# Tree attention on one core: another order for the first pairs, and copies moved between VectorE, ScalarE and GpSimd

## The chip, the cores and the metric

The kernel runs on one core of one Trainium2 chip. The metric is the device time of one execution in microseconds, the median of several runs. One core has a TensorE (PE in the profile; PEld is its loading of weights), a VectorE (DVE), a ScalarE (ACT), a GpSimd (POOL), a SyncE (SP) and 16 DMA engines. GpSimd's own DMA queue can convert fp32 to bf16 on the way. The queues of SyncE and ScalarE, called hardware queues here, are used without converting.

## The reference, cut to what matters

```python
batch, heads, seq, dim = 8, 12, 512, 64
for i in range(seq):                      # node i sees itself and its ancestors in a binary tree
    mask[i, i] = 1
    parent = i
    while parent > 0:
        parent = (parent - 1) // 2
        mask[i, parent] = 1
scores  = np.einsum('bhqd,bhkd->bhqk', Q, K) / sqrt(dim) + (1 - mask) * (-1e9)
weights = softmax(scores)
out     = np.einsum('bhqk,bhkd->bhqd', weights, V)   # fp32
```

There are 96 heads of 512 queries by 64. A node has at most nine ancestors. So a query needs its scores against the nodes near the root, and against a few blocks of keys in which its lower ancestors lie; most of the 512 by 512 scores are never computed.

## The kernel before, in words

The heads go in 48 pairs (`NP`), four pairs to a group of eight heads (`GP = 4`, `KB = 8`, 12 groups), and V in blocks of 16 heads (`VB`, 6 blocks). Group 0 has another layout of its loads than groups 1 to 11, which are called coarse in the code. A pair passes these stages:

- **Loads.** GpSimd issues them: `load_k`, `load_q`, `load_v`, each for eight heads as a rule, fp32 in memory and bf16 on the chip. Three tiles each are kept of K and Q (8 heads) and of V (16 heads). Only K and Q of heads 0 and 1 come as fp32 by the queues of SyncE and ScalarE (`first_load`, line 185) and are cast by VectorE (line 758).
- **Laying beside.** For groups 3 to 11 the two halves of K and of Q are copied so that heads of a pair lie beside each other (`lay_beside`, line 319, tiles Kbeside and Qbeside, two buffers each). A transpose then covers 128 rows. Q is always laid by GpSimd; K of groups 3, 4 and 5 by VectorE in turns 7, 10 and 14 (`K_TURN`), K of groups 6 to 11 by GpSimd.
- **Transposes** on TensorE (`T`, lines 359, 384 and 406) into the PSUM tile kqp, of which there is one, and its evacuation by VectorE (`evac`, lines 445, 453 and 459). In a coarse group two of the four transposes are of keys, two of queries, and the last two are evacuated together (line 445).
- **Scores** (`S`): the near-root tile (`scores1`) and the lower blocks (`scores2`), each with a matmul that adds the mask's codes; ScalarE takes the exponentials (lines 519 and 550).
- **Spreading V** (`spread`, line 309): V's rows are copied into the tile vt in the order in which the scores' columns stand. It has ten parts (0 to 9) for each block of V; parts 6 to 9 are the near-root tile. Three engines share these copies, by tables: `BY_VECTOR`, `BY_SCALAR`, and `spread_top` in GpSimd's program.
- **Values** (`V`, line 561) into the PSUM tile ob, of which there is one, then the reciprocal and the product on VectorE (`norm`, lines 594 and 599).
- **Stores** by GpSimd, eight heads each (`store`, line 607); the last four pairs singly (`store_pair`), the last two of them by the hardware queues.

The order on TensorE is written out: `FIRST` gives the steps of turns 0 to 5, one letter each; from then on a turn is `STV`, with an extra transpose in turn 9 (`TWICE`). `X` is a matmul on zeros that fills time, `K` and `Q` are the two halves of a transpose, `D` and `A` place the copies of that turn's tables. In turn i the scores of pair i and the values of pair i - 1 are issued; the transposes run some pairs ahead. What GpSimd does is a list made by `pool_program`; `pool` takes operations off its head as soon as a rule (`ready`) allows them to be issued. All engines work through their own instructions in order and wait for each other by semaphores.

Of the kernel before, what the change touches and what calls it, by code (L numbers as in the profile page):

```python
# [11 lines left out]
CODE_ROWS = 40  # L12
CODE_BITS = 16
NOUT = 10
BEHIND = 64
LANES = 8
COARSE = range(1, 12)
COARSE_K = range(1, 12)
BESIDE = {"K": range(3, 12), "Q": range(3, 12)}
K_BY_POOL = range(6, 12)  # L20


UNITS = (
# [101 lines left out]
def kernel(  # L125
# [59 lines left out]
    def first_load(eng, name, src):  # L185
        eng.dma_start(
            out=first[name][:, :, :, :].rearrange("p h t d -> p h (t d)"), in_=src[:, 0:2, :]
        )

    first_load(nc.sync, "K", Kr)  # L190
    nc.scalar.dma_start(out=ptile[:, :], in_=perm_dram.ap())
    first_load(nc.scalar, "Q", Qr)
# [58 lines left out]
    issued = {(name, h) for name in ("kst", "qst") for h in (0, 1)}  # L251
    qTs, kTs, kqps, obs, ets, ofs = {}, {}, {}, {}, {}, {}

    def load(kept, pool, name, size, src, h0, n):
# [52 lines left out]
            src = vst[0:32, h0:h1, UNITS[TOP + j][1], :]  # L307
            dst = vt[32 * j:32 * j + 32, h0:h1, 0, 0:w]
        return copy(out=dst, in_=src)  # L309

    def spread_top(o, h0=0, h1=VB):
        for part in range(6, 10):
            spread(nc.gpsimd.tensor_copy, o, part, h0, h1)
        for part in ((), (4, 5), (4, 5), (4, 5, 2))[min(o, 3)]:
            spread(nc.gpsimd.tensor_copy, o, part, h0, h1)

    besides = {}

    def lay_beside(copy, name, g):

        kept = (ksts if name == "K" else qsts)[g]
        to = besides[name, g] = beside.tile([P, GP, 4, 2, D], bf16, name=f"{name}beside")
        dst = to[:, :, :, :, :].bitcast(mybir.dt.uint32)
        src = kept[:, :, :, :].bitcast(mybir.dt.uint32)
        if g not in COARSE:
            src = src.rearrange("p (x a) t w -> p x t a w", a=2)
        elif name == "Q" or g in COARSE_K:
# [5 lines left out]
        copy(out=dst, in_=src)  # L333
# [284 lines left out]
            in_=ofs[i][:, a:a + n, :, :].rearrange("p h t d -> p h (t d)"),  # L618
        )

    def pool_program():

        K_BEFORE = {
            6: (load_k, 8 * KB, KB), 10: (spread_top, 5, 0, KB), 11: (store, nc.gpsimd, 5),
        }

        Q_BEFORE = {
            3: (load_k, 5 * KB, KB), 4: (load_k, 6 * KB, KB), 5: (spread_top, 3, 0, KB), 6: (spread_top, 3, KB, VB),
            9: (spread_top, 4, KB, VB), 10: (spread_top, 5, KB, VB),
        }  # L630
        ops = [
            (load_k, 2, 2), (load_q, 2, 2), (load_v, 0, 8), (load_k, 4, 4),
            (load_q, 4, 2), (load_q, 6, 2), (load_k, 8, 8), (load_q, 8, 8), (eye_order,),
            (load_v, 8, 8), (code_order, 0), (code_order, 64),
            (load_k, 16, 8), (load_q, 16, 8), (load_v, 16, 8),
            (load_k, 24, 8), (load_q, 24, 8), (load_v, 24, 8),
            (load_k, 32, 8), (spread_top, 0, KB, VB), (spread_top, 1, 0, KB),
            (load_v, 32, 8), (load_q, 32, 8), (load_k, 40, 8),
            (spread_top, 1, KB, VB),
        ]  # L640
        stored = 0
        for h in range(40, NH, KB):
            if h == 40:
                ops += [(load_v, h, KB), (load_q, h, KB)]
            else:
                ops += [(load_k, h, KB), (load_q, h, KB)]
            if h + KB < NH:
                ops.append((load_v, h + KB, KB))
            if h % VB == KB:
                ops.append((spread_top, h // VB, 0, KB))  # L650
            elif h >= 48:
                ops.append((spread_top, h // VB - 1, KB, VB))
            while KB * stored + KB + BEHIND <= h + KB:
                ops.append((store, nc.gpsimd, stored))
                stored += 1
        ops.append((spread_top, NH // VB - 1, KB, VB))
        ops += [(store, nc.gpsimd, q) for q in range(stored, NH // KB - 1)]
        ops += [(store_pair, nc.gpsimd, i) for i in (NP - 4, NP - 3)]
        for g in BESIDE["Q"]:
            if g in Q_BEFORE:  # L660
                ops.insert(ops.index(Q_BEFORE[g]), (lay_q, g))
                continue
            at = ops.index((load_q, KB * g, KB)) + 1
            behind = 0
            while behind < LANES:
                behind += {load_k: 1, load_q: 1, load_v: 1, store: 2, store_pair: 1}.get(ops[at][0], 0)
                at += 1
            ops.insert(at, (lay_q, g))
        for g in K_BY_POOL:
            before = K_BEFORE.get(g, (lay_q, g))  # L670
            ops.insert(ops.index(before), (lay_early, g))
        return ops

    def ready(op, i):

        f, args = op[0], op[1:]
        if f in (load_k, load_q):
            g = args[0] // KB - 3
            name = "K" if f is load_k else "Q"
            return (name, g) in besides if g in BESIDE[name] else done >= GP * (g + 1)  # L680
        if f in (code_order, eye_order):
            return True
        if f in (lay_q, lay_early):
# [3 lines left out]
        if f is spread_top:  # L687
            return 2 * i >= VB * (args[0] + 1 - NV)
        if f is store_pair:
            return i > args[1]  # L690
        return i >= GP * (args[1] + 1)

    BY_VECTOR = {
# [15 lines left out]
    }  # L709
    BY_SCALAR = {  # L710
        0: [(0, 8, 0, 4), (0, 1, 0, 4), (0, 4, 0, 4), (0, 5, 0, 8)],
        2: [(0, 9, 4, 8)],
        4: [(0, 1, 8, 16), (0, 2, 8, 16)],
        8: [(1, 2, 0, 8)],
        12: [(1, 2, 8, 16)],
        15: [(2, 1, 0, 8)],
        18: [(2, 1, 8, 16)],
    }

# [26 lines left out]
                out=tile[:, 0, :], lhsT=idle[:, 0:128], rhs=idle[:, :], start=True, stop=True  # L746
            )

    def lay_k(i):

        for g in BESIDE["K"]:
            if g not in K_BY_POOL and i == K_TURN.get(g, GP * g - 7):
                lay_beside(nc.vector.tensor_copy, "K", g)

    spin("s1", 9)
    for kept, name, src in ((ksts, "kst", "K"), (qsts, "qst", "Q")):
        kept[0] = loads.tile([P, KB, 4, D], bf16, name=name)
        nc.vector.tensor_copy(out=kept[0][:, 0:2, :, :], in_=first[src][:, :, :, :])
    TWICE = (9,)
    K_TURN = {3: 7, 4: 10, 5: 14}  # L760
    FIRST = ['XKSQ', 'SXXXKXQDVAT', 'SVATT', 'SVTT', 'STV', 'STVD']
    done = 1
    pool(-1)
    transpose(0)
    evac(0)
    valued = False
    for i in range(NP + 1):
        steps = FIRST[i] if i < len(FIRST) else "STVT" if i in TWICE else "SVT" if i == 8 else "STV"
        for n, step in enumerate(steps):
            if step == "S" and i < NP:  # L770
                scores1(i)
                scores2(i)
            if step == "V" and i >= 1:
                values(i - 1)
                norm(i - 1)
                valued = True
            if step == "T" and done < NP:
                transpose(done)
                evac(done)
                done += 1  # L780
                if "T" not in steps[n + 1:]:
                    lay_k(i)
            if step == "K":
                transpose(done, (0,))
            if step == "Q":
                transpose(done, (1,))
                evac(done)
                done += 1
            if step == "X":
                spin("s1" if valued else "ob", 2)  # L790
            if step == "D":
                spread_by(nc.vector.tensor_copy, BY_VECTOR, STEADY_VECTOR, i)
            if step == "A":
                spread_by(nc.scalar.copy, BY_SCALAR, STEADY_SCALAR, i)
        if "D" not in steps:
            spread_by(nc.vector.tensor_copy, BY_VECTOR, STEADY_VECTOR, i)
        if "A" not in steps:
            spread_by(nc.scalar.copy, BY_SCALAR, STEADY_SCALAR, i)
        if "T" not in steps:
            lay_k(i)  # L800
        pool(i)
        if i == NP - 1:
            store_pair(nc.sync, NP - 2)
    assert not program
# [32 lines left out]
```

## Time and profile before

| | |
|---|---|
| median of 3 runs | 132.94 us (132.73 to 133.97) |
| profiled execution: span | 131.9 us |
| profiled execution: own time | not shown apart from the span; the median lies 1.04 us above it |
| TensorE busy | 115.4 us (88%) |
| VectorE busy | 99.8 us (76%) |
| GpSimd busy | 96.0 us (73%) |
| ScalarE busy | 94.1 us (71%) |
| read from and written to HBM | 37.86 MB and 12.58 MB |
| granted TensorE clock | 0.993 |

The profile is of one execution. Times in it count from the first instruction. A line of the timeline has start, length, engine, line of the code, operation, what it writes and reads, the number of instructions merged, and in brackets the idle time before it with what ended that. In a line of the windows stand start:end, length, and for each engine the busy time with the number of instructions, then the granted clock, the busy share of the DMA engines (over 1 where packets overlap), and what they moved in GB/s.

### The profile page before, as it was taken

Reading aid. Unit: us, or ns where it says so; the run is one execution under the profiler, and the core shown is the slowest. Engines: PE = TensorE matmul, PEld = TensorE weight load, DVE = VectorE, ACT = ScalarE, POOL = GpSimd, SP = SyncE. Lnnn points to the kernel's source line nnn. Section 1 sums busy time; section 2 is a strip of 40 time slices with the busy share of each in tenths; the row PEclk is TensorE's granted clock in tenths of the full one; section 3 lists DMA queues with packets and bytes.
Section 4 is the critical chain, followed back from the end, with each engine's and each line's share of the span. In section 5 each row is a group of like instructions: output and inputs, shape, how many; then the busy total and the mean of one; then the engine's idle time right before and its main releaser. Section 6 shows DMA issues by size and latency. Waiting matters only on the chain.

```text
span 131.9 us, 4944 instructions
## 1 busy us (share of the span) xinstructions
PE 115.4 (88%) x2130; PEld 82.4 (62%) x2131; DVE 99.8 (76%) x191; ACT 94.1 (71%) x154; POOL 96.0 (73%) x147
## 2 busy tenths in 40 slices
PE   4989968899799879699999998999999999989930
PEld 1443645667566657477777776786877777856620
DVE  4339957774996897987988979879888799775460
ACT  4339345797766695778977889587888897979910
POOL 6999546049589899999999999699699998202300
PEclk9999999999999999999999999999999999999997
DMA  3999999999999999999999999999999989999991
GB/s 115 201 181 194 212 195 217 195 211 204 208 200 211 205 208 201 211 202 212 205 207 207 220 342 221 208 341 228 209 325 245 299 352 391 370 381 404 375 366 66
DMA packets 24533, 32.13 MB, mean 244 GB/s; under 512 B 944, under 2 KB 15920, under 8 KB 24512
## 3 DMA queue, kind: packets, MB, share of 16 engines
q0 software_dynamic: 23232, 30.67, 110.2%
q1 hardware_dynamic: 720, 0.70, 1.6%
q10 hardware_dynamic: 560, 0.46, 1.1%
q8 instruction: 16, 0.26, 0.7%
q14 instruction: 5, 0.04, 0.1%
HBM read 37.86 MB, written 12.58 MB: 382 GB/s over the span
## 4 chain that ended last, share of the span: by engine, by line
PE 63%; DVE 25%; ACT 6%; issue 3%; ACTq 0%
PE ob L561 18%; PE s L503 8%; PE kqp L406 8%; DVE of L599 7%; DVE kq L445 6%; PE s L508 6%; PE kqp L384 6%; PE s L528 6%; PE s L534 5%; DVE vt L309 4%; PE s L745 3%; ACT e L550 3%; ACT e L519 2%; PE kqp L359 2%; DVE kq L453 2%
## 5 line engine op out<-in xcount | busy, mean ns | idle before, releaser
L519 ACT ACTIVATE e<-s 128x1024 bf16<-128x1024 f32 x48 | 49.1, 1023 | 28.1 <-PE s L508 27.9
L309 POOL COPY vt<-vst 32x256 uint32<-32x256 uint32 (+2 forms) x70 | 36.1, 516 | 10.1 <-DMA vst<-in_V_dram 6.9
L550 ACT ACTIVATE e<-s 128x384 bf16<-128x384 f32 (+1 forms) x92 | 41.4, 505 | 0.0
L561 PE MATMUL ob<-vt,e 128*128 128x65 bf16 (+1 forms) x940 | 37.3, 197 | 3.2 <-DVE of L599 2.4
L561 PEld LDWEIGHTS <-e 128*128 128x128 bf16 (+1 forms) x960 | 31.2, 102 | 9.4 <-DVE of L599 4.8
L599 DVE TENSOR_TENSOR of<-ob,rec 128x512 f32<-128x512 f32 x44 | 30.4, 691 | 1.5
L309 DVE COPY vt<-vst 32x512 uint32<-32x512 uint32 (+4 forms) x43 | 23.2, 539 | 1.2
L594 DVE RECIPROCAL rec<-ob 128x8 f32<-128x8 f32 x47 | 9.5, 203 | 14.3 <-PE ob L561 13.5
L534 PEld LDWEIGHTS <-kq 64*128 64x128 bf16 x384 | 16.1, 110 | 6.4
L508 PE MATMUL s<-kq 64*128 64x512 bf16 x96 | 18.4, 378 | 1.3 <-DVE kq L445 1.3
L534 PE MATMUL s<-kq 64*128 64x160 bf16 (+1 forms) x384 | 17.8, 210 | 0.0
L503 PE MATMUL s<-qcoarse,codes 40*128 40x512 bf16 x88 | 17.2, 387 | 0.0
L528 PE MATMUL s<-qcoarse,codes 40*128 40x480 bf16 x88 | 16.3, 364 | 0.4 <-ACT e L550 0.2
L453 DVE COPY kq<-kqp 128x1024 bf16<-128x1024 bf16 x22 | 15.1, 687 | 2.0 <-PE kqp L384 1.3
L607 POOL DMA_DIRECT2D out_dram<-of x11 | 9.8, 893 | 8.5 <-DVE of L599 8.5
L445 DVE COPY kq<-kqp 128x2048 bf16<-128x2048 bf16 x11 | 13.5, 1224 | 2.4 <-PE kqp L406 1.8
L528 PEld LDWEIGHTS <-codes 40*128 40x128 bf16 x96 | 7.5, 95 | 9.1 <-issue 2.0
L384 PE MATMUL kqp<-mixed,Kbeside 128*128 128x128 bf16 x144 | 11.1, 220 | 1.8 <-DVE Kbeside L333 1.2
L333 POOL COPY Qbeside<-qst 128x1024 uint32<-128x1024 uint32 x9 | 9.7, 1081 | 2.6 <-DMA qst<-in_Q_dram 2.5
L406 PE MATMUL kqp<-ptile,Qbeside 128*128 128x128 bf16 x144 | 11.1, 220 | 0.4 <-DVE kq L453 0.4
L260 POOL DMA_DIRECT2D vst<-in_V_dram x12 | 10.9, 907 | 0.0
L384 PEld LDWEIGHTS <-Kbeside 128*128 128x128 bf16 x144 | 8.3, 98 | 3.2 <-DVE Kbeside L333 1.5
(45 smaller groups left out, 97.7 us busy)
## 6 DMA issues: line engine op xcount, KB each, us to landing
out_dram<-of POOLq DMA_DIRECT2D x11, 1024.0 KB, 9.9
vst<-in_V_dram POOLq DMA_DIRECT2D x12, 512.0 KB, 14.4
kst<-in_K_dram POOLq DMA_DIRECT2D x11, 512.0 KB, 12.2
qst<-in_Q_dram POOLq DMA_DIRECT2D x11, 512.0 KB, 13.2
out_dram<-ol POOLq DMA_DIRECT2D x2, 256.0 KB, 5.3
qst<-in_Q_dram POOLq DMA_DIRECT2D x3, 128.0 KB, 7.6
ol<-in_K_dram SPq DMA_DIRECT2D x1, 256.0 KB, 2.9
ol<-in_Q_dram ACTq DMA_DIRECT2D x1, 256.0 KB, 3.6
```

Source lines behind the costliest of these rows:

```text
L309: return copy(out=dst, in_=src)
L384: nc.tensor.transpose(out=dst, in_=src, identity=perm)
L406: nc.tensor.transpose(out=dst, in_=src, identity=eye[:, 0:128])
L445: return nc.vector.tensor_copy(out=dst, in_=src) if x == 3 else None
L503: nc.tensor.matmul(out=columns(g, sp[:, a, :], 0, 512), lhsT=k1code[64 * a:64 * a + CODE_ROWS, :], rhs=query_codes(i, a, 0, 0, 512), start ...
L508: nc.tensor.matmul(out=columns(g, sp[:, a, :], 0, 512), lhsT=keys(i, a, TOP), rhs=queries(i, a, 0, 512), start=False, stop=True,)
L519: nc.scalar.activation(out=dst, in_=src, func=AF.Exp, scale=scale)
L528: nc.tensor.matmul(out=columns(g, flat[:, a, :], 32, 512), lhsT=k2code[64 * a:64 * a + CODE_ROWS, :], rhs=query_codes(i, a, 1, 32, 512), s ...
L534: nc.tensor.matmul(out=columns(g, flat[:, a, :], lo, hi), lhsT=keys(i, a, TILE2[t]), rhs=queries(i, a, lo, hi), start=False, stop=t == 1,)
L550: nc.scalar.activation(out=dst, in_=src, func=AF.Exp, scale=scale)
L561: nc.tensor.matmul(out=ob[lo:hi, a, 65 * t:65 * t + 65], lhsT=e[:, a, PLACE[t], lo:hi], rhs=vt[:, head(i, a) % VB, tile_v, 0:D + 1], **flags,)
L599: nc.vector.tensor_tensor(out=dst, in0=o4[:, a:a + n, :, 0:D], in1=rec[:, a:a + n, :, :].to_broadcast([P, n, 4, D]), op=ALU.mult,)
```

## The change

It replaces the generated program of GpSimd and the tables by others:

- K and Q of heads 2 and 3 come as fp32 by the queues of SyncE and ScalarE and are cast by ScalarE; GpSimd's first load is V of heads 0 to 7, then K and Q of heads 4 to 7, four heads at a time.
- The first pairs have another order on TensorE: pair 0's values come after the scores of pair 2 instead of pair 1, and the filling matmuls behind the first are gone.
- The near-root parts (6 to 9) of the first eight heads of V are copied by GpSimd, no longer by VectorE and ScalarE.
- Part 3 of V blocks 1 and 2 goes from VectorE to ScalarE.
- K of groups 3 and 5 is laid by GpSimd instead of VectorE; K of group 4 stays on VectorE in turn 10.
- The extra transpose of turn 9 moves to turn 17, and turn 8 has the usual order.
- GpSimd's list is written out. The loads of K, Q and V of the last groups stand earlier in it, the stores later: the first store comes behind the last load of V.

```diff
-    for name, src in (("K", Kr), ("Q", Qr)):
-        first[name] = olast.tile([P, 2, 4, D], fp32, name="ol")
+    for h in (0, 2):
+        for name in "KQ":
+            first[name, h] = olast.tile([P, 2, 4, D], fp32, name="ol")
...
     nc.sync.dma_start(out=codes[0:CODE_BITS, :], in_=code_dram.ap())
+    first_load(nc.sync, "K", 2)
+    first_load(nc.scalar, "Q", 2)
...
+    POOL = (
+        "v0 k4.4 q4.4 k8 q8 v8 e c0.6.0.8 c0.7.0.8 c0.8.0.8 c0.9.0.8 x0 x64 k16 q16 v16 k24 q24 v24 "
+        "k32 t0.8 t1.0 K3 v32 q32 Q3 k40 t1.8 v40 q40 v48 t2.0 "
+        "Q4 k48 q48 v56 K5 t2.8 k56 q56 v64 Q5 t3.0 K6 k64 q64 v72 Q6 t3.8 "
+        "k72 q72 K7 Q7 v80 k80 q80 t4.0 v88 s0 K8 Q8 k88 q88 t4.8 s1 K9 Q9 t5.0 s2 K10 s3 Q10 t5.8 s4 K11 Q11 s5 s6 s7 s8 s9 s10 p44 p45 "
+    )
...
     BY_VECTOR = {
-        0: [(0, 0, 0, 8), (0, 7, 0, 8), (0, 2, 0, 8), (0, 6, 0, 8), (0, 9, 0, 4), (0, 3, 0, 8), (0, 8, 4, 8)],
-        1: [(0, 4, 4, 8)],
-        2: [(0, 1, 4, 8)],
+        0: [(0, 0, 0, 8), (0, 2, 0, 8), (0, 3, 0, 8)],
+        1: [(0, 1, 0, 8), (0, 4, 0, 8)],
         3: [(0, 4, 8, 16), (0, 5, 8, 16)],
         4: [(0, 3, 8, 16), (0, 0, 8, 16)],
-        7: [(1, 1, 0, 8), (1, 3, 0, 8)],
+        7: [(1, 1, 0, 8)],
...
     BY_SCALAR = {
-        0: [(0, 8, 0, 4), (0, 1, 0, 4), (0, 4, 0, 4), (0, 5, 0, 8)],
-        2: [(0, 9, 4, 8)],
+        0: [(0, 5, 0, 8)],
         4: [(0, 1, 8, 16), (0, 2, 8, 16)],
+        7: [(1, 3, 0, 8)],
...
-    K_TURN = {3: 7, 4: 10, 5: 14}
-    FIRST = ['XKSQ', 'SXXXKXQDVAT', 'SVATT', 'SVTT', 'STV', 'STVD']
+    EARLY = "CK CQ X K S Q D0 S A0 T D1 S T V S V T T V T T S D3 A3 T V S D4 A4 T V D5"
+    TURNS = {8: 'S T V', 10: 'S T L4 V', 17: 'S T V T'}
```

In GpSimd's list k, q, v are loads by their first head; e and x are the orders of the constants; c is one spread copy (block, part, heads); t is all of GpSimd's spread copies for eight heads of a block; K and Q lay a group beside; s and p are stores. In `EARLY`, C casts a load of heads 2 and 3 on ScalarE, and L4 lays K of group 4 on VectorE.

More of the change, by code (lines that the diff above doesn't have):

```diff
@@ L14 @@
 NOUT = 10
-BEHIND = 64
-LANES = 8
 COARSE = range(1, 12)
@@ L250 @@
     qsts, ksts, vsts = {}, {}, {}
-    issued = {(name, h) for name in ("kst", "qst") for h in (0, 1)}
+    issued = {(name, h) for name in ("kst", "qst") for h in range(4)}
     qTs, kTs, kqps, obs, ets, ofs = {}, {}, {}, {}, {}, {}
@@ L619, in store_pair @@
         )
-    def pool_program():
[L623 to L644, printed above, removed]
-            else:
[L646 to L671, printed above, removed]
@@ L747, in spin @@
             )
[L749 to L753, printed above, removed]
     spin("s1", 9)
-    for kept, name, src in ((ksts, "kst", "K"), (qsts, "qst", "Q")):
+    for kept, name in ((ksts, "kst"), (qsts, "qst")):
         kept[0] = loads.tile([P, KB, 4, D], bf16, name=name)
-        nc.vector.tensor_copy(out=kept[0][:, 0:2, :, :], in_=first[src][:, :, :, :])
-    TWICE = (9,)
@@ L760, with cast @@
-    K_TURN = {3: 7, 4: 10, 5: 14}
-    FIRST = ['XKSQ', 'SXXXKXQDVAT', 'SVATT', 'SVTT', 'STV', 'STVD']
-    done = 1
-    pool(-1)
+    def cast(copy, name, h):
+        kept = ksts if name == "K" else qsts
+        copy(out=kept[0][:, h:h + 2, :, :], in_=first[name, h][:, :, :, :])
+    cast(nc.vector.tensor_copy, "K", 0)
+    cast(nc.vector.tensor_copy, "Q", 0)
+    EARLY = "CK CQ X K S Q D0 S A0 T D1 S T V S V T T V T T S D3 A3 T V S D4 A4 T V D5"
+    TURNS = {8: 'S T V', 10: 'S T L4 V', 17: 'S T V T'}
@@ L764 @@
+    done, scored, valued = 1, 0, 0
+    pool(0)
     transpose(0)
     evac(0)
[L766 to L801, printed above, removed]
@@ L802 @@
+    for token in EARLY.split():
+        step(token)
+        if token[0] in "STVQ":
+            pool(valued)
+    for i in range(scored, NP + 1):
+        turn = "S T V" if i not in TURNS else TURNS[i]
+        for token in turn.split():
+            step(token)
+        spread_by(nc.vector.tensor_copy, BY_VECTOR, STEADY_VECTOR, i)
+        spread_by(nc.scalar.copy, BY_SCALAR, STEADY_SCALAR, i)
+        pool(valued)
         if i == NP - 1:
```

76 lines of the change are left out of this document (64 added, 12 removed), and 6 rows, old and new, of the table BY_VECTOR.

## The prediction

> **What bounds the kernel now.** I read the page first, then the windows of five stages, then the end of the timeline, then GpSimd's and ScalarE's timelines in the middle.
>
> ```profile
> span 131.9 us, 4944 instructions
> PE 115.4 (88%) x2130; PEld 82.4 (62%) x2131; DVE 99.8 (76%) x191; ACT 94.1 (71%) x154; POOL 96.0 (73%) x147
> ```
> ```profile
> 4.00:12.00 8.00, 7.34 (x70) 3.50 (x70) 3.99 (x8) 4.53 (x7) 7.94 (x13) 1.00 1.33 178
> 12.00:28.00 16.00, 13.54 (x289) 9.46 (x287) 12.79 (x25) 9.68 (x15) 6.54 (x11) 1.00 1.23 205
> 28.00:57.00 29.00, 24.96 (x471) 18.19 (x464) 23.45 (x41) 21.09 (x37) 25.25 (x41) 1.00 1.25 207
> 57.00:104.00 47.00, 46.01 (x893) 34.92 (x891) 40.65 (x76) 38.47 (x65) 42.64 (x65) 1.00 1.20 242
> 106.00:107.00 1.00, 1.00 (x28) 0.80 (x25) 0.97 (x2) 1.00 (x3) 0.99 (x1) 1.00 0.83 326
> 129.00:130.00 1.00, 0.00 (x0) 0.00 (x0) 0.00 (x0) 0.00 (x0) 0.00 (x0) 1.00 0.20 69
> ```
> In the windows the columns are start:end, length, busy time of PE, PEld, DVE, ACT and POOL, granted clock (full in all), the DMA engines' share, and GB/s. Two things run nearly without a gap. The DMA engines do from the first stage on: their share is over 1 in every long window, falls a little below only around 106, and ends at 129.2 (0.20 of the last window). And TensorE is 98% busy from 57 to 104, after losing 2.5 us before 28 and 4.0 us from 28 to 57.
>
> ```profile
> 127.65 0.35 ACTq L616 DMA_DIRECT2D out_dram<-ol  x1
> ```
> ```profile
> out_dram<-ol ACTq DMA_DIRECT2D x1, 128.0 KB, 3.0
> ```
> The last store is issued at 127.65, lands 3.0 later, and the span closes 1.2 after that. So computing sets the end, but the transfers run dry only 1.6 us after computing has finished. Computing that ended earlier would gain at most what the transfers let it.
>
> **Where the stages are coupled.** GpSimd issues every large load, spreads V, and lays Q and (from group 6) K beside each other; TensorE can't transpose a group's keys before that laying.
>
> ```profile
> 34.07 1.03 POOL L333 COPY Qbeside<-qst 128x1024 uint32<-128x1024 uint32 x1 [1.26 <-DMA qst<-in_Q_dram]
> ...
> 36.63 3.19 POOL L309 COPY vt<-vst 32x256 uint32<-32x256 uint32 x6 [0.87 <-DMA vst<-in_V_dram]
> ...
> 42.29 3.64 POOL L309 COPY vt<-vst 32x256 uint32<-32x256 uint32 x6
> ...
> 68.62 0.91 POOL L607 DMA_DIRECT2D out_dram<-of  x1
> 69.51 0.71 POOL L270 DMA_DIRECT2D kst<-in_K_dram  x1
> 70.21 0.74 POOL L270 DMA_DIRECT2D qst<-in_Q_dram  x1
> 71.00 1.03 POOL L333 COPY Kbeside<-kst 128x1024 uint32<-128x1024 uint32 x1
> 71.98 1.03 POOL L333 COPY Qbeside<-qst 128x1024 uint32<-128x1024 uint32 x1
> 72.96 0.89 POOL L260 DMA_DIRECT2D vst<-in_V_dram  x1
> 73.85 4.10 POOL L309 COPY vt<-vst 32x256 uint32<-32x256 uint32 x7
> 77.90 0.90 POOL L607 DMA_DIRECT2D out_dram<-of  x1
> 78.83 1.04 POOL L333 COPY Kbeside<-kst 128x1024 uint32<-128x1024 uint32 x1
> ```
> ```profile
> 72.38 0.62 PE L384 MATMUL kqp<-mixed,Kbeside 128*128 128x128 bf16 x8
> ...
> 81.45 0.61 PE L384 MATMUL kqp<-mixed,Kbeside 128*128 128x128 bf16 x8 [0.32 <-DVE kq L445]
> ```
> At 36.63 GpSimd waits for V of heads 24 to 31 to land. From there to the end of laying K of group 8, at 78.83 + 1.04 = 79.87, no row shows a wait: it is one chain of its own work. The rows at 72.38 and 81.45 are the first key transposes of groups 7 (pair 28) and 8 (pair 32). K of group 7 was ready at 71.00 + 1.03 = 72.03, K of group 8 at 79.87. GpSimd leads TensorE by 0.35 and 1.6 us there. That is the lead to be spent.
>
> **The change, part by part.**
>
> *K and Q of heads 2 and 3 by the hardware queues.* GpSimd no longer issues these two loads:
> ```profile
> 1.26 0.84 POOL L260 DMA_DIRECT2D kst<-in_K_dram  x1 [0.82 <-POOLq L821]
> 2.10 0.73 POOL L260 DMA_DIRECT2D qst<-in_Q_dram  x1
> ```
> The bytes read are the same, and from 4 us on the engines are already shared beyond 1, so I put the gain in transfer time at 0. The bounds: if the stage 4 to 12 moved at the next stage's rate, it would save 8 x (1 - 178/205) = 1.05 us; if fp32 destinations crowd Q of the first heads by as much, it costs the same. ScalarE's two new casts stand before its first exponential, in a stretch where its row has 4.53 busy of 8: 0. [...]
>
> *The first pairs.* Copies that stood on ScalarE ahead of the second exponential go to GpSimd; the scores of pairs 1 to 3 come sooner. But two ScalarE copies that stood ahead of pair 5's exponential now stand behind it, and pair 4's value products wait for them, with pair 6's scores queued behind those on TensorE.
> ```profile
> 25.74 1.27 ACT L309 COPY vt<-vst 32x512 uint32<-32x512 uint32 x2
> 27.03 1.02 ACT L519 ACTIVATE e<-s 128x1024 bf16<-128x1024 f32 x1
> 27.95 0.87 ACT L550 ACTIVATE e<-s 128x384 bf16<-128x384 f32 x2
> 28.81 1.02 ACT L519 ACTIVATE e<-s 128x1024 bf16<-128x1024 f32 x1
> ...
> 70.02 1.02 ACT L519 ACTIVATE e<-s 128x1024 bf16<-128x1024 f32 x1 [0.33 <-PE s L508]
> 70.94 0.87 ACT L550 ACTIVATE e<-s 128x384 bf16<-128x384 f32 x2
> 72.14 1.02 ACT L519 ACTIVATE e<-s 128x1024 bf16<-128x1024 f32 x1 [0.33 <-PE s L508]
> ```
> If pair 5's exponentials still begin at 27.03 less the 0.5 they no longer wait, their 1.9 and the copies' 1.27 end at 29.7; one value product and one score later pair 6 follows at 30.7, against 28.81: 1.9 us late. If the head start survives that far it is 0. I take the late end, because the same transposes, evacuations and normalizations must be done by pair 4 in either order.
>
> *Turns 7 to 22.* Pairs 6 to 23 took 72.14 - 28.81 = 43.3 us, 2.55 each, against 2.12 (70.02 to 72.14) when TensorE runs free: 7.3 us of stalls. The change takes K of groups 3 and 5 off VectorE and gives four of its V copies to ScalarE at 1.27/2 = 0.63 each, and takes one transpose out of turn 9, put back in turn 17. The lays cost:
> ```profile
> L333 POOL COPY Kbeside<-kst 128x1024 uint32<-128x1024 uint32 x6 | 6.3, 1044 | 1.4 <-DMA kst<-in_K_dram 1.2
> L333 DVE COPY Kbeside<-kst 128x1024 uint32<-128x1024 uint32 x3 | 2.1, 687 | 0.0
> ```
> VectorE is freed of 2 x 0.69 and four copies, some 3.5 us in all. Bounds for TensorE: 0 and 7.3; I take 3.5. Then pair 23 comes at 72.14 + 1.9 - 3.5 = 70.5, ahead of before, and asks for K of group 7 at once.
>
> *GpSimd's chain, the term that decides.* K of group 3 (1.04) now stands ahead of Q of group 3, where GpSimd waited 1.26 for a load: hidden; without that wait it costs 1.04. Behind 36.63 the new order adds, up to K of group 8: K of group 5 (1.04), loads of K and Q of group 10 (0.71 + 0.74) and of V at head 88 (0.89); the second store (0.90) leaves, and the first (0.91) only moves. Sum: +2.48. VectorE copies fewer V pieces beside it; the six copies at 42.29 took 3.64 and those at 36.63 took 3.19, so I credit 0.45 (bounds 0 and 1.2, the latter if later blocks shorten too). Net +2.0. K of group 8 is ready at 79.87 + 2.0 = 81.9, and pair 32's keys are transposed at 81.9 instead of 81.45: +0.45. Queued behind that transpose on TensorE are pair 26's value products and pair 28's scores, and ScalarE waits for those. K of group 7 has +1.04 - 0.91 = +0.13: 72.2, the same as before. So the 3.5 us won in the turns before are waited away at groups 7 and 8. Behind K of group 8 the stores are spread thinner and K of group 9 keeps step.
>
> *The stores.* All later, behind the last V load; they fill the engines while loads are done. The dip around 106 (share 0.83) should fill: 0.17 of one or two microseconds, so 0.2 to 0.4 us, but only in the transfers, which don't set the end here. After 57 TensorE has no stall to give, except at the group boundary of pair 32, whose wait now swallows the normalization wait beside it: -0.25.
>
> *Sum.* 131.9 + 0.45 - 0.25 = 132.1 of span. The profiled execution's own time isn't shown apart; the median of the runs is 132.94, 1.04 above the span. Forecast: 133.1 us. Bounds from the terms: start of the chain -1.05 to +1.05, credit -0.75 to +0.45, early pairs up to +1.9 if nothing is won behind.
>
> **Rivals.**
> *Fast: transfers quicken, GpSimd's chain starts sooner.* For it: 178 against 205 GB/s in the early stage, and the dip. V of heads 24 to 31 lands 1.05 earlier, the credit is 1.2: K of group 8 at 79.87 + 2.48 - 1.2 - 1.05 = 80.1, 1.35 sooner at pair 32, and the transfers, 1.05 + 0.4 sooner, allow it. Time 132.94 - 1.4 = 131.5. Against it: no engine was idle early.
>
> *Slow: the late copies of pair 4 aren't made up.* If the stalls of turns 7 to 22 come from evacuations rather than from the copies moved, pair 23 comes at 72.14 + 1.9 = 74.0. From 72.2 on, when K of group 7 is there, lateness counts in full: 132.94 + 1.9 = 134.8. For it: one transpose fewer ahead from turn 9 to 17, so each group's large evacuation has less time. [...]
>
> *GpSimd isn't the gate* (the later K loads find room): only the transfers bound it, 132.94 less the 0.4 of the dip: 132.5. Against it: leads of 0.35 and 1.6 us against +2.0.
>
> **Chances.** Forecast 0.36; no gate 0.14; fast 0.25; slow 0.25. A change within 1% (131.6 to 134.3) is about what a measurement can't tell from none. Faster 0.25, same 0.5, slower 0.25. The forecast alone holds 132.2 to 134.0; with the rivals the range is 131.2 to 135.0.
>
> **What would show it.** Right: the value products of pair 4 wait for ScalarE's copies; TensorE is ahead before pair 28 and then waits 1 us or more for GpSimd's lays of groups 7 and 8; pair 32's keys are transposed between 81 and 83; DMA share without a dip near 106, ending at 129. Wrong: those transposes before 80.5 (fast), pair 23's exponential after 73 (slow), or idle DMA engines before 125.

## The result, and the profile after

The changed kernel takes 138.11 us (median of 4 runs, 137.53 to 138.37), the kernel before beside it 132.97. The ratio is 1.035 with a 95% interval of 1.030 to 1.040: it is 5 us slower, and the forecast of 133.1 with a range up to 135.0 was wrong. The profiled execution took 137.53 us. Here and below medians are of all executions, while ratios leave out those over 1.5% slower than the fastest of the same kernel, which matters most for a_sw, sw_a4 and b3: 4 of 10, 5 of 12 and 6 of 12 are left out there, and the medians of all would give 1.014, 1.012 and 1.008.

The page of the changed kernel first: its span, its busy times, the granted clock and the DMA engines' share in 40 slices of 3.4 us.

```profile
span 135.6 us, 4934 instructions
PE 117.4 (87%) x2123; PEld 84.1 (62%) x2123; DVE 95.5 (70%) x181; ACT 96.4 (71%) x156; POOL 97.5 (72%) x150
PEclk9985556999999999999999999999999999999995
DMA  3999999999999999999999999999999999994573
```

The last two rows tell most of it. The granted clock, full in every window that the prediction showed of the kernel before, falls to half from the third slice to the seventh. And the DMA engines, busy to the end before, run dry at the end: the transfers now wait for computing. The windows of the changed kernel show both (columns as in the prediction: TensorE's busy time first, the granted clock, DMA share and GB/s last).

```profile
8.00:9.00 1.00, 0.00 (x0) 0.00 (x0) 0.00 (x0) 0.00 (x0) 0.00 (x0) 1.00 1.34 225
9.00:10.00 1.00, 0.00 (x0) 0.00 (x0) 0.00 (x0) 0.35 (x1) 0.00 (x0) 0.67 1.45 198
12.00:16.00 4.00, 3.75 (x44) 2.09 (x42) 2.64 (x4) 2.99 (x4) 3.78 (x8) 0.50 1.16 212
22.00:23.00 1.00, 1.00 (x22) 0.83 (x18) 0.00 (x0) 1.00 (x2) 0.00 (x0) 0.50 1.14 212
23.00:24.00 1.00, 0.89 (x29) 0.72 (x27) 0.49 (x2) 0.53 (x1) 0.00 (x0) 1.00 1.14 207
104.00:108.00 4.00, 3.76 (x78) 2.80 (x76) 3.58 (x8) 2.76 (x7) 3.96 (x5) 1.00 1.03 403
124.00:128.00 4.00, 3.88 (x79) 2.59 (x79) 1.80 (x4) 3.80 (x8) 1.38 (x2) 1.00 0.35 129
```

At 8 to 9 us no engine does anything but the DMA engines. ScalarE's and TensorE's timeline names what is waited for, and the DMA issues between 1.7 and 2.4 us tell how long that took to land (last column).

```profile
9.65 0.62 ACT L733 CAST kst<-ol 128x512 bf16<-128x512 f32 x1 [3.64 <-DMA ol<-in_K_dram]
10.32 0.64 PE L354 MATMUL kqp<-ptile,kst 128*64 128x128 bf16 x8 [3.30 <-ACT kst L733]
```
```profile
ol<-in_K_dram SPq DMA_DIRECT2D x1, 256.0 KB, 7.7
```

K of heads 2 and 3, issued by SyncE at 1.94, takes 7.7 us and lands at 9.6. In the kernel before the same heads came by GpSimd's queue, half as many bytes on the chip, and TensorE took them at 7.66:

```profile
kst<-in_K_dram POOLq DMA_DIRECT2D x1, 128.0 KB, 4.2
```
```profile
7.66 0.41 PE L359 MATMUL kqp<-ptile,kst 128*64 128x128 bf16 x8
```

TensorE stands for 3.30 us, the clock falls in the midst of that (0.67 in the window from 9 to 10), and the same eight transposes take 0.64 instead of 0.41. The clock is half until 23 us, though TensorE is busy 3.75 of the 4 us from 12 to 16, and as much of the next 4. Heads 2 and 3 are pair 1, so pair 0 does not need this load: its scores are late because the written order (`X K S Q`) puts the key transposes of pair 1 ahead of them. That holds in both kernels, and no run put the scores first. The start of the near-root exponential of some pairs, from the timelines of ScalarE, shows how the loss grows and shrinks (the last three kernels are experiments below):

| pair | before | after | a_sw | a_warm | b4 |
|---|---|---|---|---|---|
| 0 | 8.66 | 11.97 | 8.77 | 11.03 | 8.65 |
| 4 | 23.93 | 29.39 | 23.15 | 25.63 | 25.05 |
| 6 | 28.81 | 36.05 | 30.54 | 32.81 | 29.88 |
| 16 | 56.48 | 60.09 | 56.60 | 57.82 | 54.36 |
| 23 | 72.14 | 76.03 | 72.54 | 73.77 | 70.31 |
| 32 | 92.40 | 96.55 | 93.80 | 94.50 | 90.17 |
| 47 | 124.04 | 128.69 | 126.32 | 127.02 | 123.01 |

The changed kernel is 3.3 us late at pair 0, 7.2 at pair 6, 3.9 at pair 23 and 4.65 at the last pair.

### The profile page after: what moved, and what is told of

Same layout as the page of the kernel before. It is cut to its first block, busy times and chain, and to the rows that moved or that the text cites. A ratio compares the mean times of both kernels' runs of the same rounds, so it can differ in the third digit from the quotient of the medians.

```text
span 135.6 us, 4934 instructions
## 1 busy us (share of the span) xinstructions
PE 117.4 (87%) x2123; PEld 84.1 (62%) x2123; DVE 95.5 (70%) x181; ACT 96.4 (71%) x156; POOL 97.5 (72%) x150
## 4 chain that ended last, share of the span: by engine, by line
PE 60%; DVE 22%; ACT 6%; DMA 6%; issue 3%; ACTq 0%; SPq 0%
PE ob L556 16%; DVE kq L440 7%; PE s L498 7%; PE s L503 7%; PE kqp L401 7%; PE kqp L379 7%; PE s L523 7%; PE s L529 6%; DMA ol<-in_K_dram 6%; DVE of L594 5%; DVE vt L310 3%; ACT e L545 3%; PE kqp L354 2%; DVE kq L448 2%; DVE rec L589 1%
## 5 line engine op out<-in xcount | busy, mean ns | idle before, releaser
L310 POOL COPY vt<-vst 32x256 uint32<-32x256 uint32 (+2 forms) x74 | 37.3, 504 | 9.9 <-DMA vst<-in_V_dram 6.6
L556 PEld LDWEIGHTS <-e 128*128 128x128 bf16 (+1 forms) x960 | 32.0, 103 | 9.0 <-DVE of L594 2.8
L529 PEld LDWEIGHTS <-kq 64*128 64x128 bf16 x384 | 17.1, 114 | 7.5 <-issue 2.1
L503 PE MATMUL s<-kq 64*128 64x512 bf16 x96 | 19.4, 398 | 2.5 <-DVE kq L440 2.0
L310 DVE COPY vt<-vst 32x512 uint32<-32x512 uint32 (+1 forms) x35 | 19.8, 567 | 1.0
L529 PE MATMUL s<-kq 64*128 64x160 bf16 (+1 forms) x384 | 18.7, 217 | 0.0
L271 POOL DMA_DIRECT2D kst<-in_K_dram x11 | 7.7, 704 | 5.5 <-PE kqp L379 4.0
```

Source lines behind the costliest of these rows:

```text
L503: nc.tensor.matmul(out=columns(g, sp[:, a, :], 0, 512), lhsT=keys(i, a, TOP), rhs=queries(i, a, 0, 512), start=False, stop=True,)
L529: nc.tensor.matmul(out=columns(g, flat[:, a, :], lo, hi), lhsT=keys(i, a, TILE2[t]), rhs=queries(i, a, lo, hi), start=False, stop=t == 1,)
L556: nc.tensor.matmul(out=ob[lo:hi, a, 65 * t:65 * t + 65], lhsT=e[:, a, PLACE[t], lo:hi], rhs=vt[:, head(i, a) % VB, tile_v, 0:D + 1], **flags,)
```

## The experiments

All of them, as ratios to the kernel before on the same chip. The ratios are what is compared.

| kernel | median, us | ratio (95% interval) |
|---|---|---|
| changed kernel | 138.11 | 1.035 (1.030 to 1.040) |
| a_sw: loads of heads 2 and 3 by GpSimd again | 135.04 | 1.008 (1.003 to 1.013) |
| a_warm: more filling matmuls in the wait | 135.94 | 1.019 (1.012 to 1.027) |
| a_v0late: GpSimd's queue starts later | 136.65 | 1.025 (1.018 to 1.032) |
| b_hw: kernel before with the hardware loads alone | 140.58 | 1.055 (1.048 to 1.063) |
| a_a4: pair 4's ScalarE copies earlier | 136.36 | 1.022 (1.017 to 1.028) |
| sw_a4: a_sw and a_a4 together | 135.24 | 1.008 (1.004 to 1.012) |
| sw_a4_st: and VectorE's part 0 later | 133.71 | 0.998 (0.994 to 1.002) |
| b1: and GpSimd lays K earlier | 133.57 | 0.998 (0.995 to 1.002) |
| b2: b1 and more filling matmuls | 133.85 | 1.000 (0.997 to 1.004) |
| b3: b1 and K, Q of heads 4 to 7 ahead of V | 134.91 | 0.999 (0.995 to 1.003) |
| b4: b2 and more lays earlier | 133.54 | 0.997 (0.994 to 1.001) |
| a_b4: b4 with the hardware loads | 134.30 | 1.005 (1.001 to 1.008) |

My theory: GpSimd's loads, V first, hold the DMA engines while the two hardware loads are under way; TensorE waits for these and its clock falls. The rivals: GpSimd's new list and later stores, or the new order of the first pairs.

**a_sw, the loads back on GpSimd's queue.**

```diff
-    first_load(nc.sync, "K", 2)
-    first_load(nc.scalar, "Q", 2)
...
-        "v0 k4.4 q4.4 k8 q8 v8 e ...
+        "k2.2 q2.2 v0 k4.4 q4.4 k8 q8 v8 e ...
...
-    EARLY = "CK CQ X K S Q ...
+    EARLY = "X K S Q ...
```

> The changed kernel, but K and Q of heads 2 and 3 come by GpSimd's queue again, as its first two loads, without casts on ScalarE. Theory (the two hardware loads land late because GpSimd's queue takes the shared DMA engines; TensorE waits 3.3 us for K and its clock drops to 0.5 until 23 us): the wait and the slow clock go, pair 0's exponential starts near 8.7 instead of 11.97, and the time falls by 4 to 6 us, to 132 to 134. Rival one (GpSimd's new list and later stores cost the time): pair 0 comes early but pair 32 does not, time stays at 136 to 138. Rival two (the new order of the first pairs, with copies of pair 4 behind pair 5's exponential, costs it): pair 6 still comes near 36, time 136 to 138.

Measured: 1.008, so 2.7% of the 3.5% are gone, some 3.5 us. Pair 0 comes at 8.77. So the hardware loads are the main cause. The kernel's next wait shows now:

```profile
28.52 0.96 PE L554 MATMUL ob<-vt,e 128*128 128x65 bf16 x16 [2.02 <-ACT vt L308]
32.14 1.20 PE L554 MATMUL ob<-vt,e 128*128 128x65 bf16 x20
```
```profile
28.00:29.00 1.00, 0.48 (x8) 0.43 (x7) 0.00 (x0) 0.47 (x1) 0.45 (x2) 0.62 1.16 217
34.00:35.00 1.00, 1.00 (x12) 0.49 (x8) 0.32 (x1) 0.59 (x1) 1.00 (x2) 0.50 1.25 208
35.00:36.00 1.00, 1.00 (x32) 0.90 (x28) 0.29 (x1) 1.00 (x3) 0.91 (x2) 0.96 1.17 217
```

TensorE waits 2.02 us for ScalarE's two copies for pair 4, and here the clock falls behind that wait and is half until 35 (twenty value matmuls take 1.20; in the changed kernel at full clock, at 25.64, they take 0.79). Whether it falls differs from one execution to the next: two of ten had a clock of 0.994 and 0.995 and took 133.2 and 133.3 us, the others 0.953 to 0.967 and 134.7 to 136.9. Yet that wait is not what this profiled execution ends late by: at pair 23 it is only 0.4 us behind the kernel before, at the last pair 2.3. In between it loses some 0.67 us at the end of each of three groups: from pair 23 to 24, 31 to 32 and 35 to 36 it takes 3.0 us, the kernel before 2.33. The first of them, on VectorE and TensorE:

```profile
70.79 1.18 DVE L308 COPY vt<-vst 32x512 uint32<-32x512 uint32 x1
72.01 1.23 DVE L438 COPY kq<-kqp 128x2048 bf16<-128x2048 bf16 x1
73.28 0.61 PE L377 MATMUL kqp<-mixed,Kbeside 128*128 128x128 bf16 x8 [0.43 <-DVE kq L438]
```

A copy of V stands ahead of the large evacuation, for which TensorE waits. The runs sw_a4 and sw_a4_st try the two waits one after the other.

**a_warm, the wait without the slow clock.** `X` becomes `X8`: eight filling matmuls in place of two ahead of the first transpose that needs the late load. (The expectation calls it pair 0's; it is pair 1's, which stands ahead of pair 0's scores.)

> The changed kernel with eight filling matmuls instead of two before the first key transpose of pair 0, so that TensorE has work through most of the wait for the late loads; the loads are as in the changed kernel. It tells the wait from the clock. Theory, if the clock carries most of it: granted clock stays near 1.0 from 8 to 24, pair 0 still starts near 12, pair 6 comes near 32 to 33 instead of 36, and the time is 134 to 136. If the wait carries it: clock full, yet 137 to 138. If the idle time isn't what lowers the clock: clock again 0.5 and 138.

```profile
10.03 0.41 PE L354 MATMUL kqp<-ptile,kst 128*64 128x128 bf16 x8 [1.01 <-ACT kst L733]
30.99 0.75 PE L556 MATMUL ob<-vt,e 128*128 128x65 bf16 x16 [2.02 <-ACT vt L310]
```
```profile
12.00:20.00 8.00, 6.41 (x130) 4.38 (x130) 6.81 (x12) 6.32 (x9) 7.12 (x10) 1.00 1.24 208
28.00:36.00 8.00, 5.98 (x102) 4.11 (x98) 3.11 (x8) 4.70 (x9) 6.63 (x11) 0.79 1.24 207
```

As the theory has it for the clock: idle for 1.01 instead of 3.30, TensorE keeps its full clock, the key transposes take 0.41, and pair 4 comes at 25.63 instead of 29.39. Against a_sw's 23.15 that splits the 6.2 us of lateness at pair 4 into 3.8 of clock and 2.5 of waiting (0.3 of the 3.8 are a load that landed a little sooner in this execution, after 7.4 us). At the end only 1.6% (2.1 us) is won. Here the clock falls behind the second wait (0.79), which it did not do in the changed kernel; how much of the gain that takes is not shown.

**a_v0late, GpSimd's queue later.** Only the order of one constant (`e`) goes ahead of V in GpSimd's list; it waits for a small load until 3.70, so V is issued at 4.36 instead of 1.26.

> The changed kernel with GpSimd's ordering of the small constant moved ahead of the first load of V, so that its queue starts some 2 us later; all else as in the changed kernel, the hardware loads of K and Q of heads 2 and 3 included. Theory (crowding by GpSimd's queue): with the engines free longer, K and Q of heads 2 and 3 land near 6 to 7 instead of 8.3 and 9.6, TensorE's wait falls from 3.3 to about 1 us or less, the clock stays higher, and the time is 133 to 136. Rival (the hardware queues' loads are slow in themselves, or casts on ScalarE are what is late): they still land after 8 and the time is 138 or more.

The same load of K of heads 2 and 3, issued at 1.95, and what TensorE then waits for:

```profile
ol<-in_K_dram SPq DMA_DIRECT2D x1, 256.0 KB, 4.6
```
```profile
6.61 0.62 ACT L733 CAST kst<-ol 128x512 bf16<-128x512 f32 x1
12.37 0.41 PE L354 MATMUL kqp<-ptile,kst 128*64 128x128 bf16 x8 [1.35 <-DMA kst<-in_K_dram]
14.14 0.64 PE L354 MATMUL kqp<-ptile,qst 128*64 128x128 bf16 x8 [1.36 <-DMA qst<-in_Q_dram]
```

4.6 us instead of 7.7, the cast without a wait at 6.61, pair 0 at 8.66 as before. The hardware queue is not slow in itself: it was crowded out. But GpSimd's loads are now late by the same 3 us, TensorE waits 1.35 and 1.36 us for K and Q of heads 4 to 7, and the clock falls there instead (0.50 from 14 to 20). The time is 1.025, 136.65 us, between what the theory (up to 136) and the rival (138 or more) had: the mechanism was right, but the wait was moved rather than removed. Bytes needed at 7.7 and bytes needed at 12 pass over the same 16 engines (the queues' shares of them in the changed kernel, 81, 21 and 14% from 5 to 8, stand further below); the order between them has to fit.

**b_hw, this part of the change alone.** In the kernel before, K and Q of heads 2 and 3 go to the hardware queues with ScalarE's casts; nothing else is touched.

> The kernel before, with one part of the change alone: K and Q of heads 2 and 3 come as fp32 by the hardware queues and are cast by ScalarE, and GpSimd leaves these two loads out. Theory: this part alone brings the wait at pair 0 and the lower clock, so the time rises from 133 to 136 to 138.5. Rivals (GpSimd's list, or the order of the first pairs): this part is harmless, 132.5 to 133.5.

```profile
10.63 0.64 PE L362 MATMUL kqp<-ptile,kst 128*64 128x128 bf16 x8 [3.22 <-ACT kst L763]
15.68 3.17 PE L748 MATMUL ob<-idle 128*128 128x512 bf16 x6
18.78 0.64 PE L362 MATMUL kqp<-ptile,kst 128*64 128x128 bf16 x8
```

140.6 us, worse than the whole change and above what I expected. The wait is the same (3.22). What I had not counted: the older order issues filling matmuls in turn 1, and at half clock six of them take 3.17 us on a path that is late already. In the kernel before, at full clock, the row in their place (five of the six are on record) is:

```profile
11.17 1.68 PE L745 MATMUL ob<-idle 128*128 128x512 bf16 x5 [0.16 <-issue]
```

So the new order of the first pairs, without those, probably saves some of what the hardware loads cost; no run has that order alone.

**a_a4 and sw_a4, pair 4's copies.**

```diff
-    ... T T S D3 A3 T V S D4 A4 T V D5"
+    ... T T A4 S D3 A3 T V S D4 T V D5"
```

> The changed kernel with its hardware loads of K and Q of heads 2 and 3, and only the two ScalarE copies of pair 4 moved ahead of pair 4's scores. It tells whether the late copies cost the changed kernel anything of their own. Theory (the two causes add): 138.1 less the wait of 2.0 at pair 4, so 135.5 to 136.5. Rival (what is late at pair 4 in the changed kernel is late for the loads of the first heads anyway): 137.5 to 138.2.

> K and Q of heads 2 and 3 by GpSimd's queue again, and besides the two ScalarE copies that pair 4's values wait for stand ahead of pair 4's scores, where ScalarE is idle for 5 us, instead of behind pair 5's exponentials. Theory (a second step of the loss: TensorE waits 2.0 us for these copies, and its clock falls to 0.5 behind that wait in most runs): against the 135.04 of the kernel with GpSimd's loads alone, the wait of 2.0 and the slow clock behind it go, pair 6 comes near 27.5 instead of 30.5, and the time is 131 to 132.5, at or below the kernel before. Rival (the time is set later, by the laying of K by GpSimd or the transfers): pair 6 comes early, the stretch behind it gives all of it back by pair 32, and the time stays at 133.5 to 135.

a_a4 came out as the theory said: 1.022 against 1.035, so 1.7 us less. Its profiled execution is one of the two longest of six (137.64 us), and K of heads 2 and 3 landed still later in it:

```profile
ol<-in_K_dram SPq DMA_DIRECT2D x1, 256.0 KB, 9.5
```
```profile
12.18 0.64 PE L354 MATMUL kqp<-ptile,kst 128*64 128x128 bf16 x8 [4.82 <-ACT kst L733]
```

At pair 4 that execution waits 1.23 us instead of 2.02, and for a copy of VectorE's, no longer of ScalarE's.

sw_a4 was a miss: 1.008, no better than a_sw, though the wait of 2.02 is gone and pairs 4 to 6 take 4.9 us instead of 7.4. Its profiled execution took 136.05 us, more than its median of 135.24, so it shows how the gain can be lost and not how much is lost as a rule. Early, TensorE waits 2.04 and 0.67 us for K and Q of heads 4 to 7, and the clock is half from 13 to 19. Late, on VectorE and TensorE:

```profile
97.07 2.12 DVE L308 COPY vt<-vst 32x512 uint32<-32x512 uint32 x1
99.22 1.22 DVE L438 COPY kq<-kqp 128x2048 bf16<-128x2048 bf16 x1
...
100.50 0.61 PE L377 MATMUL kqp<-mixed,Kbeside 128*128 128x128 bf16 x8 [1.37 <-DVE kq L438]
```
```profile
102.00:103.00 1.00, 1.00 (x16) 0.57 (x15) 0.38 (x2) 0.00 (x0) 0.96 (x3) 0.50 1.04 414
```

One copy of V, 0.42 us in the changed kernel while GpSimd is idle (at 114.79), takes 2.12 beside GpSimd's work, the large evacuation behind it is late, TensorE waits 1.37, and the clock falls once more. It is the same chain as at the group ends of a_sw.

**sw_a4_st, that copy out of the way.** `STEADY_VECTOR = {0: 0, 1: 1, 3: 3}` becomes `{1: 1, 2: 0, 3: 3}`.

> As the first of these three, and besides VectorE's copies of V's part 0, for V blocks 3 to 5, come two turns later, so that they don't stand ahead of the large evacuation at a group's end. Theory (GpSimd's lays of K and Q slow a VectorE copy that runs beside them from 0.42 to 1.1 to 1.5 us, and where that copy stands ahead of the large evacuation, TensorE waits 0.67 us at the group's start): the gaps from pair 23 to 24, 31 to 32 and 35 to 36 fall from 3.0 to 2.33 each, and the time is 1 to 2 us under that of the first. Rival (these boundaries wait for something else, or the slow copy meets another evacuation instead): within 0.5 us of the first.

The time is 1.0% (1.3 us) better than that of sw_a4, 0.998 against 1.008: the size that was expected. The place was only half right: of the gaps, that from pair 31 to 32 is 2.34 and from 35 to 36 2.61, but that from 23 to 24 is still 2.94, because TensorE now waits for the lays of GpSimd.

```profile
71.46 0.62 PE L377 MATMUL kqp<-mixed,Kbeside 128*128 128x128 bf16 x8 [0.76 <-POOL Kbeside L326]
81.30 0.62 PE L377 MATMUL kqp<-mixed,Kbeside 128*128 128x128 bf16 x8 [1.18 <-POOL Kbeside L326]
```

The second row is pair 32's key transpose, waiting for K of group 8: the gate that the prediction had put at 81.9.

**b1, b2 and b3, lays, fillers, K ahead of V.** b1 moves K6, K7 and K8 forward in GpSimd's list; b2 adds fillers (`D0 S A0 X4 T D1 X S`); b3 instead puts `k4.4 q4.4` ahead of `v0`, with fillers and later copies in the first pairs (`S X2 T X S D0 A0 D1`).

> The third of the kernels before (loads of heads 2 and 3 by GpSimd, earlier ScalarE copies for pair 4, VectorE's part 0 two turns later), and besides GpSimd lays K of groups 6, 7 and 8 earlier: K of group 6 ahead of the V copies that stood ahead of it, K of group 7 ahead of two loads, K of group 8 ahead of the V copies and loads that stood ahead of it. Theory (with the other waits gone GpSimd's chain is the gate, as the prediction had it: TensorE waits 0.19, 0.76 and 1.18 us for these lays): the waits go and the time falls by 1 to 2 us, to 131.5 to 133. Rival (the V copies and loads that come later by it hold TensorE instead, or the lays meet VectorE's copies): 133.2 to 134.5.

> As the one before, with four filling matmuls ahead of pair 2's key transpose and two ahead of pair 2's value of the order, where TensorE waits 0.3 to 2 us for K and Q of heads 4 to 7. Theory (short waits there lower the clock from about 12 to 20 us in some executions, which is the spread of 2 us between them): clock near 0.99 in all, spread under 1 us, time 0.5 to 1.5 us below the one before. Rival (the clock falls for other reasons, or the fillers stand in the way of the work): the same time or up to 1 us more.

> As the first of these three, but GpSimd issues K and Q of heads 4 to 7 ahead of V of heads 0 to 7, with V's copies by VectorE and ScalarE put behind pair 2's scores, and four filling matmuls between the scores of pairs 0 to 2. It tells what V ahead of K and Q costs. Theory: pair 2's exponential comes near 12.5 to 13.5 instead of 14.3 to 16, the clock stays full, and the time is 1 us or more below the first. Rival (V's rows then come late and pair 0's values hold TensorE): as the first, or up to 1.5 us more.

None moved the time: 0.998, 1.000 and 0.999, so all three theories missed. b2's profiled execution shows why. The fillers did hold the clock (0.976 to 0.997 over its executions, 0.963 to 0.985 in b1), but not the spread, which stayed 2.5 us instead of under 1. The execution was 1.6 us ahead of b1 at pair 31, at 87.17 against 88.73. Then it met the next gate of the same chain, K of group 9, and the clock fell behind it:

```profile
90.10 0.62 PE L377 MATMUL kqp<-mixed,Kbeside 128*128 128x128 bf16 x8 [2.62 <-POOL Kbeside L326]
```
```profile
92.00:93.00 1.00, 1.00 (x13) 0.52 (x10) 0.97 (x2) 0.64 (x1) 0.90 (x3) 0.50 1.08 401
```

b3 has pair 2 at 13.13 as expected (14.64 in b1) and meets the same gate (a wait of 2.61 at 90.55). Its executions spread most, from 132.9 to 137.5, and their median is 134.91, 1.3 us over b1's. Whether V first costs anything by itself is left open.

**b4 and a_b4, all these waits mended.** b4 is b2 with K7, K9, K10 and K11 further forward; a_b4 is the same with the hardware loads of heads 2 and 3 and eight fillers.

> The kernel with GpSimd's loads, earlier copies for pair 4, part 0 later and filling matmuls, and besides GpSimd lays K of groups 7, 9, 10 and 11 ahead of the V copies and stores that stood ahead of them. Theory (the last gate is GpSimd's chain: TensorE waited 0.66 us for K of group 7 and 2.62 for K of group 9, and the clock fell behind the second): both waits go, and with the 1.9 us of lead that this kernel had at pair 31 the time is 131 to 132.5, under the kernel before by over 1%. Rival (the transfers set the end by then, or lays stand in the way of V's copies): 133 to 134.

> The changed kernel with the hardware loads of K and Q of heads 2 and 3 kept, and all the other mends of the kernel before it in this call, with eight filling matmuls in the wait for these loads. The two differ in the loads of heads 2 and 3 alone. Theory: pair 0 comes near 11 instead of 8.3, and the hardware loads cost what is left of that at the end: 1 to 2.5 us more than the other, 132.5 to 135. Rival (with everything else mended the late start is made up before the end): within 0.5 us of the other.

In b4 the timeline shows only one wait of TensorE over 0.25 us behind 54 us (0.60 at 115.98; the kernel before has 0.59 at 117.02), and its computing ends earlier than in the kernel before: the last store is issued at 126.63 instead of 127.65. Yet the time is 0.997 (0.994 to 1.001), the rival's. Its last windows and its last store:

```profile
120.00:124.00 4.00, 3.88 (x79) 2.60 (x74) 1.80 (x4) 3.79 (x8) 1.80 (x3) 1.00 1.02 392
124.00:128.00 4.00, 1.37 (x31) 1.01 (x28) 2.02 (x6) 0.80 (x3) 0.38 (x1) 0.85 1.00 385
```
```profile
126.63 0.35 ACTq L609 DMA_DIRECT2D out_dram<-ol  x1
```

The DMA engines are full to 128 us, and nearly so in the kernel before (0.97 from 124 to 128); 50.4 MB over the span of 130.6 us are 386 GB/s, much as in these windows. So I take the transfers for what bounds this execution. No run with fewer bytes was made: the floor is read from the windows, not tried. It is also one of the shortest executions (132.54 us, with a median of 133.54), and what the longer ones lose has no trace. a_b4 is at 1.005: with everything else mended the hardware loads still cost 0.7% (1.0 us), with K landing after 7.2 us and pair 0 at 10.86 in its profiled execution. So no version here beats the kernel before by more than the measurement can tell; b4 takes 3.6% less than the changed kernel.

## Why the prediction was wrong, step by step

**K and Q of heads 2 and 3 by the hardware queues: the step that failed.** It was put at 0, with bounds of 1.05 on both sides. Undone, it gives back 2.7% (3.5 us); done alone, it costs 5.5% (7.4 us). I priced the transfer as bandwidth: the same bytes, over engines that are shared beyond 1 anyway. But TensorE does not wait for the bytes in sum; it waits for those 256 KB. Their landing time against their first use, 1.94 + 7.7 = 9.6 against 7.66, was the number to work out. The profile before has rows that bear on it: 4.2 us for this load as the first in GpSimd's queue, 2.9 us for the hardware load of K issued at 0.74, and 7.3 to 9.4 us for the large loads in flight behind it. No row gave the 7.7 itself, but these had to be asked for, and I set the term to 0 without it. What the runs showed in its place is crowding. The issues of the changed kernel between 1 and 3 us, beside the queues' shares of the DMA engines between 5 and 8:

```profile
ol<-in_K_dram SPq DMA_DIRECT2D x2, 256.0 KB, 5.3
kst<-in_K_dram POOLq DMA_DIRECT2D x1, 256.0 KB, 10.4
```
```profile
q0 software_dynamic: 616, 0.32, 80.6%
q1 hardware_dynamic: 172, 0.17, 21.2%
q10 hardware_dynamic: 95, 0.09, 13.8%
```

GpSimd's queue has 81% of the engines' time (packets overlap, so the sum is over 1) while the two hardware queues, which carry what TensorE waits for, have 21% and 14%. That the engines are shared stood in the prediction's own windows (1.33 from 4 to 12); the mistake was to draw from it that nothing changes.

**ScalarE's casts: 0.** Wrong too, though small: I looked at whether ScalarE was free, not at what stands behind the cast. It stands between the landing and the transpose: from 9.65 to 10.32, 0.67 of the 3.30.

**What was never priced: the clock.** The prediction said that the clock is full in all windows and asked of no wait what it does to the clock. The filling matmuls that the change takes away had no price either. At pair 4 the clock is some 3.8 of 6.2 us. At the end a_warm, which keeps the clock there, gains only 2.1 us and still stands at 135.94, above the range.

**The first pairs: 1.9 us late at pair 6.** Right in mechanism: TensorE waits 2.02 us for ScalarE's copies. With GpSimd's loads (a_sw) pair 6 comes at 30.54, and 30.7 was forecast, but that near a hit is in part luck: pair 5's exponential began at 25.39 instead of 26.5, and the half clock behind the wait took about 0.7 of that back (pairs 5 to 6 take 5.15 us in a_sw and 4.42 at full clock in the changed kernel). What it costs at the end is not settled: moving the copies gives 1.3% (1.7 us) in a_a4, where the loads are late, and nothing in sw_a4.

**Turns 7 to 22: 3.5 us won.** Right in size: the changed kernel goes from 7.2 late at pair 6 to 3.9 late at pair 23, so 3.3; in b4 those 17 pairs take 40.4 instead of 43.3, so 2.9. A late kernel does not catch up by itself: b_hw, which has the old program there, is 6.8 late at pair 6 and still 6.3 at pair 23. Which of the moved lays, copies and transposes wins the time is not separated.

**GpSimd's chain, K of group 8 at 81.9.** Right as a chain, but not the gate it was taken for, since TensorE itself came later. In the changed kernel:

```profile
82.30 1.04 POOL L328 COPY Kbeside<-kst 128x1024 uint32<-128x1024 uint32 x1
84.96 0.62 PE L379 MATMUL kqp<-mixed,Kbeside 128*128 128x128 bf16 x8
```

Laid at 83.3, 1.4 later than forecast, and taken at 84.96 without a wait. Where the first losses are mended it is the gate: in sw_a4_st TensorE takes it at 81.30, after 1.18 of waiting, and in b2 the same chain holds it 2.62 at the next group. The slow rival was right on its sign (pair 23 after 73), but it had the lateness start at pair 4, not at pair 0. The last sign of being wrong came true too: the DMA engines are idle before 125 (share 0.28 from 124 to 125).

**The stores and the transfers.** Right that the dip near 106 fills (1.03 from 104 to 108). Right too, as far as the windows of b4 show, that transfers are a floor under quicker computing. In the changed kernel that floor is not reached, since computing comes so late.

**From span to time.** 1.04 was too little: later executions of the kernel before show 1.7 to 1.9 between the two (133.11 with a span of 131.3). That moved the sum by less than 1 us.

## What to carry to other kernels

For a load that is moved to another queue, don't ask only whether the bytes fit: work out when that load lands, behind everything else that is then in flight, and set it against the first use. Of every wait of TensorE, and of short ones in a row, ask what it does to the clock; filling matmuls in the wait can hold it (a_warm kept 1.00 from 12 to 20 and gained 2.1 us by them; b2 held 0.976 to 0.997 over its executions, and gained nothing at the end). When an early loss is mended, look for the next gate (here copies, then GpSimd's lays, then the transfers) before counting the gain.

## What the runs showed of the hardware that I had not expected

- **The clock after a wait.** It fell after idle times of 3.30 (changed kernel), 2.62 (b2) and 1.37 us (sw_a4), and not after 1.01 (a_warm) or 1.08 (b1, at 90.12). After the same 2.02 it fell in a_sw and a_warm and not in the changed kernel. In b1 it was half from 14 to 17 behind three waits of 0.46, 0.91 and 0.47 us between 11 and 14. So the length of one wait does not decide it, and what does these runs leave open. How long it stayed half can be estimated from windows of one microsecond: those wholly inside or outside the stretch have 0.50 or 1.00, so a mean of 0.67 is taken as 0.66 us at half clock. In b2, whose first and last such windows stand here, that is 0.66 + 2 + 0.76 = 3.4 us; in sw_a4 it is 3.4 too, in a_sw 0.76 + 6 + 0.08 = 6.8, in the changed kernel 0.66 + 13 = 13.7.
```profile
91.00:92.00 1.00, 1.00 (x15) 0.48 (x14) 0.96 (x3) 0.00 (x0) 0.88 (x4) 0.67 1.23 335
94.00:95.00 1.00, 1.00 (x23) 0.87 (x22) 0.69 (x1) 0.15 (x1) 0.96 (x3) 0.62 1.13 256
```
  Against the 3.4 of b2 and sw_a4 that is two times as long in a_sw, four times in the changed kernel, and three times in b_hw (10.2); why, these runs leave open. Nor did busy time alone bring the clock back at once: in the changed kernel it stayed half with TensorE busy 12.19 of the 13 us from 10 to 23.
- **A VectorE copy beside GpSimd.** The copy of 32 rows of V takes 0.42 us each of the four times that GpSimd is idle (114.79 to 123.46 in the changed kernel), and up to 2.12 beside GpSimd's work (sw_a4, at 97.07); in the changed kernel the mean is 0.567, and 0.564 in the kernel before, so the two lays moved to GpSimd did not slow these copies in the mean:
```profile
L310 DVE COPY vt<-vst 32x512 uint32<-32x512 uint32 (+1 forms) x35 | 19.8, 567 | 1.0
```
  Not all of GpSimd's work lengthens it: of those in the changed kernel's timeline, the copies at 91.80 and 99.25 took 1.18 and 1.46, each beside a lay of Q (1.04 from 91.66, 1.05 from 99.38); that at 87.56, beside GpSimd's copies of V, took 0.42, and those at 108.23 and 110.34, beside the issues of stores, 0.41 and 0.42, and even that at 72.17, beside a lay of K from 72.22, took 0.41. What lengthens the long ones is not shown: no run separates GpSimd's copies from its DMA issues beside it. It matters where the copy stands ahead of an evacuation.
- **A hardware load's landing time is not a constant.** The same 256 KB took 4.6 us in a_v0late, where GpSimd's queue starts 3.1 us later, and 8.0 in b_hw. In a_b4, a_warm, the changed kernel and a_a4 it took 7.2, 7.4, 7.7 and 9.5, with the same order of GpSimd's first loads in all four; that spread of over 2 us is between executions and has no cause in the record.
